# Eight routed experts: pairs of experts in turn, transposes a step late, outputs by 128 slots, weights in two rings

## The chip, the cores and the metric

The kernel runs on one core of a Trainium2 chip. The metric is device time in microseconds; lower is better. The unmodified kernel took 2508.5 us in the median of three runs (2505.13 to 2510.0). Engines are named as in the profile: PE (matmul), PEld (its weight loads), DVE, ACT, POOL, and SP, whose queue issues the loads of weights from HBM.

## The reference, cut to what matters

The program is a two-layer block followed by a second block of other kinds of layers. The change touches one part, the mixture of experts of 256 tokens with 1024 features:

```
logits = h @ w_router;  top_val, top_idx = lax.top_k(logits, 2);  top_w = softmax(top_val)
gates = sum(one_hot(top_idx, 8) * top_w[..., None], axis=-2)
for e in range(8):
    y = (silu(h @ w_gate[e]) * (h @ w_up[e])) @ w_down[e]      # 1024 -> 3584 -> 1024
    out = out + gates[..., e:e+1] * y
```

All weights are fp32. The eight experts have 8 x 3 x 1024 x 3584 x 4 bytes = 352.3 MB, and each byte is read once.

## The kernel before, in words

The router sorts the experts by how many tokens chose them (`sort`) and gives each place p of 0 to 7 a fixed number of slots, `CAPS` = 96, 64, 96, 64, ... A branch on the largest count covers the case that a place overflows; in these inputs it isn't taken. `gather` copies the tokens of some places into slots, with one-hot matrices as matmul operands. Place 0 is always expert 0, whose weights stand at a known address; the addresses of the others are read at run time, after the sort.

Weights come as 42 blocks of 1 MiB per expert, 128 partitions by 2048 fp32. The first 28 hold gate and up columns, in four steps (8, 8, 8 and 4 blocks), and the last 14 hold the down projection. `Ahead` issues the loads on SP in the order of use, and `next` keeps ten blocks loaded or on the way (L239-244). A block has one of ten homes in turn (L227): eight are tiles of two pools with four buffers each ("raw" and "hl", which the other stages use for weights too), loaded in one piece of 1 MiB (L230); two are four units each of the general pool of 52 units of 128 x 512, loaded in four pieces of 256 KB (L235). A load waits on SP until PE has read the block that had its home before.

`expert` works on one place at a time. A group is 32 slots, so a place has three groups or two. In a step, PE multiplies the group's slots by four column tiles of the block: two tiles of gate columns into partitions 0 to 63 of a bank, two of up columns into 64 to 127 (L977). The first two groups have banks of the pool "mm", the third one of the pool "ax"; each pool has four. Then, for each group, ACT takes silu of the gate half (L983), DVE multiplies by the up half (L984), PE transposes 64 x 128 pieces (L990), and ACT or DVE copies the result to a unit (L994, L996), which is the down projection's operand (L1010). At the end ACT and DVE copy the outputs to Y (L1018, L1020), PE multiplies Y by the transposed gate matrix pT, eight matmuls of fp32, and DVE adds to the stream x (L1026). `experts` takes the places in sets, 0, then 1 to 3, 4 and 5, 6 and 7, and gathers the next set within the down projection before it. Pieces of the second block's preparation (`block2_context`) are hung on steps of the places 6 and 7 (`todo`).

A scheduler sets the order on each engine from the program's order, priorities and free buffers. Each engine then runs in that order.

Of the kernel before, what the change touches and what calls it, by code (L numbers as in the profile page):

```python
# [8 lines left out]
F32 = mybir.dt.float32  # L9
F32R = mybir.dt.float32r  # L10
# [3 lines left out]
AF = mybir.ActivationFunctionType  # L14
ALU = mybir.AluOpType
AX = mybir.AxisListType
# [14 lines left out]
RAWB, HLB = 4, 4  # L31
# [107 lines left out]
class Weights:  # L139


    def __init__(self):
        self.at, self.items, self.size = {}, [], 0
# [68 lines left out]
class Ahead:  # L212


    def __init__(self, K, off, homes=10, depth=10):
        self.K, self.off, self.loaded, self.used = K, off, [], 0
        self.homes, self.depth = homes, depth
        self.n = K.wts.experts()[1] // (P * CH)

    def fill(self, n):  # L220
        K = self.K
        while len(self.loaded) < min(n, NE * self.n):
            i = len(self.loaded)
            p, c = divmod(i, self.n)
            o = self.off[p] + c * P * CH
            src = K.a["wts"][bass.ds(o, P * CH)].rearrange("(p n) -> p n", p=P)
            home = (i + self.homes - 8) % self.homes  # L227
            if home > 1:
                t = K.wp.tile([P, CH], F32, name=K.nm("raw"), tag="raw" if home % 2 else "hl", bufs=RAWB if home % 2 else HLB)
# [9 lines left out]
    def next(self):  # L239
        i = self.used  # L240
        self.used += 1
        self.fill(i + self.depth)
        out, self.loaded[i] = self.loaded[i], None
        return out


class Kern:
# [578 lines left out]
    def moe(self, x):  # L826
# [68 lines left out]
        ahead = Ahead(self, [first] * NE)  # L895
        held = ahead.fill(8)
# [7 lines left out]
        with tc.If(n > 0):  # L904
            self.experts(x, hth, htl, srt, Ahead(self, begins, 2, 3), 0)
            self.experts(x, hth, htl, srt, Ahead(self, begins, 2, 3), 1)
            for u in [rt[:, 0]] + self.cx.u + held:
                nc.vector.tensor_copy(u[:, :1], u[:, :1])
        self.experts(x, hth, htl, srt, ahead)
# [31 lines left out]
    def experts(self, x, hth, htl, srt, ahead, over=None):  # L941
# [7 lines left out]
        nxt = None  # L949
        for i, places in enumerate(sets):  # L950
            if nxt is None:
                with self.tc.high_priority(offset=self.hp if over is None else 0):
                    nxt = self.gather(places, caps, base, hth, htl, srt)
            cur, nxt = nxt, None
            for p in places:
                last = p == places[-1] and i + 1 < len(sets)
                for s in self.expert(x, *cur[p], ahead):
                    if over is None and (p, s) in todo:
                        self.block2_context(*todo[p, s])
                    if s == 3 and last:  # L960
                        nxt = self.gather(sets[i + 1], caps, base, hth, htl, srt)

    def expert(self, x, slots, xg, pT, ahead):

        nc = self.nc
        groups = slots // GS
        ge = lambda g: slice(g * GS, g * GS + GS)
        hT = []
        for s, (a, w, kc) in enumerate(steps()):
            pss = [self.psm() if g < 2 else self.psx() for g in range(groups)]  # L970
            for k0 in range(0, KD, kc):
                blocks = ahead.next()
                for k in range(k0, k0 + kc):
                    for g in range(groups):
                        for q in range(4):
                            o = ((k - k0) * 4 + q) * w
                            self.nc.tensor.matmul(pss[g][q * GS:(q + 1) * GS, :w], xg(k, g),  # L977
                                                  blocks[o // 512][:, o % 512:o % 512 + w], start=k == 0,
                                                  stop=k == KD - 1, tile_position=(0, q * GS))
            nb, hs = w // P, [None] * groups  # L980
            for g in range(groups):
                sg, ht = self.tmp()[64:, :w], self.tmp()[64:, :w]
                nc.scalar.activation(sg, pss[g][:64, :w], AF.Silu)  # L983
                nc.vector.tensor_mul(ht, pss[g][64:, :w], sg)  # L984
                if g % 2 == 0:
                    pt, u = self.psx(), self.unit(name="hT")
                    n = min(groups - g, 2) * nb * 64
                at = (g % 2) * nb * 64
                for b in range(nb):
                    nc.tensor.transpose(pt[:, at + b * 64:at + b * 64 + 64], ht[:, b * P:(b + 1) * P],  # L990
                                        self.ident[64:, 64:])
                if g % 2 or g == groups - 1:
                    if g < 2:
                        nc.scalar.activation(u[:, :n], pt[:, :n], AF.Copy)  # L994
                    else:
                        nc.vector.tensor_copy(u[:, :n], pt[:, :n])  # L996
                hs[g] = u[:, at:at + nb * 64]
            for c in range(2):
                for b in range(nb):
                    hT.append([h[:, b * 64 + c * GS:b * 64 + c * GS + GS] for h in hs])  # L1000
            yield s
        ya, yb = self.psm(), self.psx() if groups > 2 else None
        y = [(ya, ya, yb)[g][:, (g % 2) * 256:(g % 2) * 256 + 256] for g in range(groups)]
        for k0 in range(0, EDIM // P, 2):
            blocks = ahead.next()
# [7 lines left out]
        Y = [self.unit(name="Y") for _ in range(2)]  # L1013
        for g in range(groups):
            for q in range(4):
                dst, src = Y[q // 2][ge(g), (q % 2) * 256:(q % 2) * 256 + 256], y[g][q * GS:(q + 1) * GS]
                if q % 2:
                    nc.scalar.activation(dst, src, AF.Copy)  # L1018
                else:
                    nc.vector.tensor_copy(dst, src)  # L1020
# [6 lines left out]
        yield len(steps())  # L1027

    def gather(self, places, caps, base, hth, htl, srt):

        nc = self.nc
        io = self.c["iota"]
# [3 lines left out]
        pg = self.unit(name="pg")[:, :2 * n].rearrange("p (t s) -> p t s", t=2)  # L1036
        for p in places:
            r, c = RANKS[p], caps[p]
            pos = srt[:, 4:6, r:r + 1]
            if base[p]:  # L1040
                pos = self.small(2)[:, :, None]
                nc.vector.tensor_scalar(pos, srt[:, 4:6, r:r + 1], -float(base[p]), None, op0=ALU.add)
            for dst, row in ((pr, 0), (pg, 2)):
                for t in range(2):
                    nc.vector.tensor_scalar(dst[:, t, at[p]:at[p] + c], io[:, :c], pos[:, t], srt[:, row + t, r:r + 1],
                                            op0=ALU.is_equal, op1=ALU.mult)
# [14 lines left out]
        out = {}  # L1061
        for i, p in enumerate(places):
            c = caps[p]
            if i % 2 == 0:
                ps, pT = self.psx(), self.unit(name="pT")
                two = places[i:i + 2]
            for t in range(2):
                nc.tensor.transpose(ps[:c, (i % 2) * T + t * P:(i % 2) * T + (t + 1) * P], pg[:, t, at[p]:at[p] + c], self.ident)
            o = slice((i % 2) * T, (i % 2) * T + T)
            nc.vector.tensor_copy(pT[:c, o], ps[:c, o])  # L1070
            out[p] = (c, lambda k, g, a=at[p]: xg[k][:, a + g * GS:a + g * GS + GS], pT[:, o])
        return out
# [744 lines left out]
```

## Time and profile before

| | us |
|---|---|
| median of three runs | 2508.5 |
| the profiled execution | 2513.52 |
| its span, first to last instruction | 2511.7 |
| PE busy in the span | 2389.0 |
| DVE, ACT, POOL busy | 1124.6, 812.1, 96.3 |

The page gives busy times, and a busy PE is not one at its peak, since matmuls overlap. What limits a stage is read from the chain of waits and from the share of the DMA engines by stretches: at 1.0 all 16 have packets all the time. The mean granted TensorE clock of the execution is 0.978, where 1.00 is the upper of two levels, 2.4 GHz, and 0.50 the lower. Names such as mm and ax are banks that matmuls write, raw is a block of weights, whl the split weights of the other stages, xg gathered tokens, hT the transposed hidden values.

### The profile page before, as it was taken

To read this page: it belongs to the slowest core of one execution; us is meant where nothing else is said; L and a number is where in the kernel's file an instruction comes from. 1 tells how busy PE (TensorE), PEld (TensorE's weight loads), DVE (VectorE), ACT (ScalarE), POOL (GpSimd) and SP (SyncE) were. 2 spreads that over 40 slices of the span, in tenths; PEclk is the share of its full clock that TensorE was granted. 3 is DMA by queue.
4 is the path that set the end of the run, shared out by engine and by line. 5 is a ranking of instruction groups with operands and counts; after the bars stand their busy time and mean duration, and the time that the engine had idled before them with its cause. 6 is when DMAs were issued, how large, how long until landed. Compare 5 with 4: busy or idle time off the path is not lost.

```text
span 2511.7 us, 47630 instructions
## 1 busy us (share of the span) xinstructions
PE 2389.0 (95%) x20181; PEld 1708.9 (68%) x20181; DVE 1124.6 (45%) x2262; ACT 812.1 (32%) x1372; POOL 96.3 (4%) x96
## 2 busy tenths in 40 slices
PE   8999999979989999999999998999899999898998
PEld 6788888743533535354343688878788888778998
DVE  5475545721101011111111256966764454786884
ACT  5544433611000010100101255332442342464663
POOL 0000001000000000000011100000100000101000
PEclk9999999989999999999999999999899999998999
DMA  8468787469999999999999821111222322222552
GB/s 307 175 239 291 275 290 259 161 255 361 348 409 408 390 404 398 411 397 405 381 395 405 320 84 51 42 55 66 90 74 103 117 80 88 89 101 68 193 186 93
DMA packets 113341, 581.80 MB, mean 232 GB/s; under 512 B 12727, under 2 KB 12983, under 8 KB 54368
## 3 DMA queue, kind: packets, MB, share of 16 engines
q1 hardware_dynamic: 111456, 572.74, 60.0%
q0 software_dynamic: 1664, 5.93, 0.7%
q8 instruction: 160, 2.62, 0.4%
q14 instruction: 61, 0.50, 0.1%
HBM read 575.48 MB, written 3.15 MB: 230 GB/s over the span
## 4 chain that ended last, share of the span: by engine, by line
PE 66%; DMA 4%; DVE 4%; issue 2%; ACT 2%; POOL 1%; SPq 0%; DVEq 0%; ACTq 0%; POOLq 0%
PE mm L302 32%; PE mm L977 14%; PE ax L302 6%; PE mm L1010 5%; DMA raw<-in_wts 4%; PE ax L977 4%; PE ax L1010 2%; PE ax L990 1%; DVE whl L359 0%; DVE t L984 0%; PE ax L1741 0%; ACT t L983 0%; DVE x L1140 0%; DVE t L421 0%; SPq L230 0%
## 5 line engine op out<-in xcount | busy, mean ns | idle before, releaser
L302 PE MATMUL mm<-h,whl 128*128 128x256 f32 (+2 forms) x3280 | 718.6, 314 | 14.7 <-ACT whl L358 12.2
L302 PEld LDWEIGHTS mm<-h,whl 128*128 128x128 f32 (+1 forms) x3280 | 537.1, 189 | 79.8 <-issue 23.7
L302 PE MATMUL mm<-l,whl 128*128 128x256 f32 (+2 forms) x1640 | 510.6, 313 | 0.0
L977 PE MATMUL mm<-raw,xg 128*32 128x512 f32 (+1 forms) x4096 | 488.4, 546 | 5.9 <-DMA raw<-in_wts 5.9
L359 DVE TENSOR_TENSOR whl<-raw,whl 128x1024 fp32r<-128x1024 f32 (+4 forms) x314 | 367.6, 1177 | 250.9 <-ACT whl L358 250.6
L358 ACT ACTIVATE whl<-raw 128x1024 fp32r<-128x1024 f32 (+4 forms) x314 | 318.6, 1021 | 292.7 <-PE mm L302 261.5
L977 PEld LDWEIGHTS mm<-raw,xg 128*32 128x32 f32 x4096 | 152.4, 111 | 256.9 <-issue 213.0
L302 PEld LDWEIGHTS mm<-l,whl 128*128 128x128 f32 (+1 forms) x1640 | 308.2, 188 | 20.0 <-issue 0.3
L1010 PE MATMUL mm<-raw,hT 128*32 128x256 f32 x3584 | 253.1, 385 | 10.7 <-DMA raw<-in_wts 10.6
L302 PE MATMUL mm<-fh,whl 128*128 128x256 f32 (+1 forms) x1056 | 236.1, 318 | 0.0
L984 DVE TENSOR_TENSOR t<-mm,t 64x512 f32<-64x512 f32 (+1 forms) x64 | 39.8, 627 | 436.0 <-ACT t L983 435.7
L1010 PEld LDWEIGHTS mm<-raw,hT 128*32 128x32 f32 x3584 | 135.2, 111 | 94.9 <-DMA raw<-in_wts 19.9
L983 ACT ACTIVATE t<-mm 64x512 f32<-64x512 f32 (+1 forms) x64 | 33.8, 534 | 498.0 <-PE mm L977 470.4
L302 PEld LDWEIGHTS mm<-fh,whl 128*128 128x128 f32 x1056 | 174.2, 188 | 21.5 <-issue 4.2
L977 PE MATMUL ax<-raw,xg 128*32 128x512 f32 (+1 forms) x1024 | 173.5, 541 | 0.0
L302 PE MATMUL mm<-fl,whl 128*128 128x256 f32 (+1 forms) x528 | 167.2, 317 | 0.0
L1020 DVE COPY Y<-mm 32x256 f32<-32x256 f32 x32 | 13.3, 416 | 225.7 <-PE mm L1010 218.7
L1010 PE MATMUL ax<-raw,hT 128*32 128x256 f32 x896 | 111.3, 379 | 0.0
L302 PEld LDWEIGHTS mm<-fl,whl 128*128 128x128 f32 x528 | 98.9, 187 | 7.7
L302 PE MATMUL mm<-f,whl 128*128 128x256 f32 (+1 forms) x732 | 97.8, 290 | 1.4 <-ACT f L358 1.4
L302 PEld LDWEIGHTS mm<-f,whl 128*128 128x128 f32 x732 | 91.0, 188 | 5.5 <-ACT f L358 2.0
L977 PEld LDWEIGHTS ax<-raw,xg 128*32 128x32 f32 x1024 | 48.3, 110 | 63.2 <-issue 56.6
(447 smaller groups left out, 2495.7 us busy)
## 6 DMA issues: line engine op xcount, KB each, us to landing
raw<-in_wts SPq DMA_DIRECT2D x458, 1024.0 KB, 7.1
raw<-in_wts SPq DMA_DIRECT2D x268, 256.0 KB, 9.0
raw<-in_wts SPq DMA_DIRECT2D x8, 768.0 KB, 4.5
raw<-in_wts SPq DMA_DIRECT2D x12, 512.0 KB, 3.4
raw<-in_wts SPq DMA_DIRECT2D x8, 384.0 KB, 3.0
raw<-in_wts SPq DMA_DIRECT2D x4, 576.0 KB, 3.7
spill<-x POOLq DMA_DIRECT2D x8, 256.0 KB, 3.3
x<-spill POOLq DMA_DIRECT2D x8, 256.0 KB, 4.0
```

The lines of the kernel that those rows point to most:

```text
L302: self.nc.tensor.matmul(out, lhsT, rhs, start=start, stop=stop)
L358: self.nc.scalar.activation(hi, src, AF.Copy)
L359: self.nc.vector.tensor_sub(lo, src, hi.bitcast(F32))
L977: self.nc.tensor.matmul(pss[g][q * GS:(q + 1) * GS, :w], xg(k, g), blocks[o // 512][:, o % 512:o % 512 + w], start=k == 0, stop=k == KD - ...
L983: nc.scalar.activation(sg, pss[g][:64, :w], AF.Silu)
L984: nc.vector.tensor_mul(ht, pss[g][64:, :w], sg)
L990: nc.tensor.transpose(pt[:, at + b * 64:at + b * 64 + 64], ht[:, b * P:(b + 1) * P], self.ident[64:, 64:])
L1010: self.nc.tensor.matmul(y[g][q * GS:(q + 1) * GS], hT[k][g], blocks[o // 512][:, o % 512:o % 512 + 256], start=k == 0 and g != 1, stop=k = ...
L1020: nc.vector.tensor_copy(dst, src)
```

## The change

- Places are taken in pairs (0, 1), (2, 3), (4, 5), (6, 7). The four steps of both alternate (`passes`), in the first pair with place 1 a step behind; the two down projections follow one another. The blocks are loaded in this order (`loads`).
- Blocks are kept in the two rings of four only. The early loads, before the branch, are eleven instead of eight; blocks 8 to 10 go to units. `next` keeps eight blocks ahead.
- The second group's gate and up halves change places in the bank (r = q ^ 2), so that the hidden values of groups 0 and 1 fill one tile of 128 partitions. It is transposed by 128 x 128 matmuls, and the transposes of a step stand behind the matmuls of the next one.
- Outputs of the places are collected in tiles of 128 slots (640 slots, five tiles). `combine` makes the gate matrix of a tile, turns it into a gain per slot and a 0/1 matrix, scales Y, splits it into a high and a low half of type fp32r, and multiplies both, 16 matmuls of one pass.

```diff
-RAWB, HLB = 4, 4
+RAWB, HLB, AHEAD = 4, 4, 3
-        ahead = Ahead(self, [first] * NE)
-        held = ahead.fill(8)
+        pairs = [(p, p + 1) for p in range(0, NE, 2)]
+        ring = lambda i: None if 8 <= i < 8 + AHEAD else ("raw", "hl")[(i - AHEAD * (i >= 8)) % 2]
+        ahead = Ahead(self, [first] * NE, loads(passes(pairs)), ring, 8)
+        held = ahead.fill(8 + AHEAD)
...
+def passes(pairs):
+    out = []
+    for i, pair in enumerate(pairs):
+        n = len(steps())
+        if len(pair) == 1:
+            out += [(pair[0], s) for s in range(n)]
+        else:
+            lag = 1 if i == 0 else 0
+            a, b = pair
+            for s in range(n + lag):
+                out += [(a, s)] * (s < n) + [(b, s - lag)] * (s >= lag)
+        out += [(p, None) for p in pair]
+    return out
...
-        todo = {(6, 0): (1,), (6, 1): (2,)}
-        for k in range(0, KD, 2):
-            todo[divmod(27 + k // 2, 4)] = (3, [k, k + 1])
-        sets = ([0], [1, 2, 3], [4, 5], [6, 7]) if over is None else [[p, p + 1] for p in range(0, NE, 2)]
...
+            todo = {(7, 0): [(1,)], (6, 2): [(2,)], (7, 2): [(3, (0, 1))], (6, 3): [(3, (2, 3))], (7, 3): [(3, (4, 5))],
+                    (6, None): [(3, (6, 7))]}
...
+        for i, (p, s) in enumerate(passes(sets)):
+            mine = next(j for j, places in enumerate(sets) if p in places)
+            if s is not None:
+                ps = self.gate_up(p, s, caps[p] // GS, xgs[p], ahead)
+                new = self.hidden(s, caps[p] // GS, ps, hT.setdefault(p, []))
+            else:
+                new = None
+                for part in self.down(p, caps[p] // GS, hT[p], ahead):
+                    if part == 1 and after:
+                        after()
+                        after = None
+                y = part
+            if after:
+                after()
+            after = new
+            if s is None:
+                hT.pop(p)
+                self.collect(y, at[p], caps[p] // GS, Y)
+                if p == sets[mine][0] and mine + 1 < len(sets):
+                    xgs = {**xgs, **self.gather(sets[mine + 1], caps, base, hth, htl, srt)}
+                xgs = {q: v for q, v in xgs.items() if q != p}
+                end = at[p] + caps[p] if p == NE - 1 else at[p + 1]
+                while done < end // P or (p == NE - 1 and done in Y):
+                    self.combine(done, x, Y.pop(done), caps, base, at, srt)
+                    done += 1
...
+            gate, up = (slice(64, P), slice(0, 64)) if g == 1 else (slice(0, 64), slice(64, P))
+            nc.scalar.activation(sg[up], pss[g][gate, :w], AF.Silu)
+            nc.vector.tensor_mul(ht[up], pss[g][up, :w], sg[up])
...
+                    if both:
+                        nc.tensor.transpose(pt[:, b * P:b * P + P], ht[:, bs], self.ident)
                     else:
+                        nc.tensor.transpose(pt[:, b * 64:b * 64 + 64], ht[64:, bs], self.ident[64:, 64:])
...
+        nc.vector.tensor_reduce(gs, ps[:n, :T], axis=AX.X, op=ALU.add)
+        nc.vector.tensor_scalar(pT, ps[:n, :T], 0.0, None, op0=ALU.is_gt)
+        yh = [self.unit(F32R, "yh")[:n] for _ in range(2)]
+        yl = [self.unit(F32R, "yl")[:n] for _ in range(2)]
+        for h, l, y in zip(yh, yl, Y):
+            nc.scalar.activation(h, y[:n], AF.Copy, scale=gs)
+            nc.vector.scalar_tensor_tensor(l, y[:n], gs, h.bitcast(F32), op0=ALU.mult, op1=ALU.subtract)
...
-                self.mm(ps[:, q * T:(q + 1) * T], Y[m // 4][:slots, (m % 4) * P:(m % 4 + 1) * P], pT[:slots])
+                self.mm(o, yh[m // 4][:, ms], pT, start=True, stop=False)
+                self.mm(o, yl[m // 4][:, ms], pT, start=False, stop=True)
             nc.vector.tensor_add(u, ps, u)
```

On SP's queue, around the branch, before: the last early load, the reads of the sort's result (place), the branch, and the first pieces behind it.

```order
L230 DMA raw_5332<-in_wts 128x2048
L899 TENSOR_LOAD place
L897 TENSOR_LOAD place
L899 TENSOR_LOAD place x6
L904 COMPARE_AND_BRANCH
L235 DMA raw_5434<-in_wts 128x512
```

And after the change; five more rows like the first, and the last early load of 1 MiB, stand ahead of these.

```order
L235 DMA raw_5345<-in_wts 128x512
L235 DMA raw_5346<-in_wts 128x512
L235 DMA raw_5347<-in_wts 128x512
L235 DMA raw_5352<-in_wts 128x512
L235 DMA raw_5353<-in_wts 128x512
L235 DMA raw_5354<-in_wts 128x512
L235 DMA raw_5355<-in_wts 128x512
L925 TENSOR_LOAD place
L927 TENSOR_LOAD place x7
L932 COMPARE_AND_BRANCH
```

Twelve pieces for the blocks 8 to 10 moved ahead of the reads and the branch; the rows behind it in the file are those of the branch that isn't taken.

On PE, the end of the first expert's second step, before: t is the hidden values of one group, ax the bank that its transposes write, and raw_25518 the next step's first block.

```order
L977 MATMUL mm_25563<-raw_25504,xg_25396 32x512 x4
L977 MATMUL ax_25564<-raw_25504,xg_25396 32x512 x4
L990 MATMUL ax_25693<-cst,t_25690 128x64 x4
L977 MATMUL mm_25719<-raw_25518,xg_25381 32x512
L990 MATMUL ax_25693<-cst,t_25700 128x64 x4
L977 MATMUL mm_25719<-raw_25518,xg_25381 32x512 x3
L990 MATMUL ax_25712<-cst,t_25709 128x64 x4
L977 MATMUL mm_25720<-raw_25518,xg_25381 32x512 x4
```

And after: ht_25800 is the hidden values of groups 0 and 1 of the step before, ht_25806 those of group 2, and the block behind them is place 1's first.

```order
L1024 MATMUL mm_25810<-raw_25812,xg_25690 32x512 x4
L1024 MATMUL ax_25811<-raw_25812,xg_25690 32x512 x4
L1051 MATMUL ax_25934<-cst,ht_25800 128x128 x4
L1053 MATMUL ax_25941<-cst,ht_25806 128x64 x4
L1024 MATMUL mm_25948<-raw_25826,xg_25664 32x512 x4
L1024 MATMUL mm_25949<-raw_25826,xg_25664 32x512 x4
```

Three sets of four transposes became two, and they belong to the step before the one that just ended.

On PE, where place 6 begins, before: the first two groups' last block of the step, the combine of place 5 (pT and Y), and then the third group's matmuls of the step's first block, raw_30605.

```order
L977 MATMUL mm_30805<-raw_30739,xg_30492 32x512
L977 MATMUL mm_30806<-raw_30738,xg_30492 32x512
L977 MATMUL mm_30806<-raw_30739,xg_30492 32x512
L302 MATMUL ax_30789<-pT_28707,Y_30779 128x256 x2
L302 MATMUL ax_30793<-pT_28707,Y_30779 128x256 x2
L302 MATMUL ax_30797<-pT_28707,Y_30780 128x256 x2
L302 MATMUL ax_30801<-pT_28707,Y_30780 128x256 x2
L977 MATMUL ax_30807<-raw_30605,xg_30466 32x512 x4
L977 MATMUL ax_30807<-raw_30623,xg_30466 32x512 x4
```

And after, where place 6 begins: the end of the down projection before it and its own first two blocks.

```order
L1077 MATMUL mm_30362<-raw_30471,hT_29942 32x256 x16
L1024 MATMUL mm_30623<-raw_30489,xg_30290 32x512 x4
L1024 MATMUL mm_30624<-raw_30489,xg_30290 32x512 x4
L1024 MATMUL ax_30625<-raw_30489,xg_30290 32x512 x4
L1024 MATMUL mm_30623<-raw_30507,xg_30290 32x512 x4
L1024 MATMUL mm_30624<-raw_30507,xg_30290 32x512 x4
L1024 MATMUL ax_30625<-raw_30507,xg_30290 32x512 x4
```

The third group's matmuls now follow each block, and the combine stands elsewhere, within a down projection.

## Rows read from the trace of the kernel before

**Rows 1.** Busy time by stretches (us, instructions), granted clock, DMA share, GB/s.

```profile
core 0: us, PE busy (x) PEld busy (x) DVE busy (x) ACT busy (x) POOL busy (x), PEclk, DMA share, GB/s
543.00:690.00 147.00, 146.38 (x1722) 64.39 (x1718) 19.76 (x43) 14.80 (x29) 0.00 (x0) 1.00 0.92 352
690.00:840.00 150.00, 139.61 (x1488) 53.63 (x1484) 15.57 (x26) 13.27 (x25) 0.00 (x0) 0.99 1.02 409
840.00:920.00 80.00, 79.30 (x1089) 38.96 (x1084) 8.23 (x16) 5.54 (x13) 0.00 (x0) 1.00 1.00 392
...
1106.00:1220.00 114.00, 104.99 (x1147) 46.55 (x1139) 14.80 (x32) 11.79 (x25) 0.00 (x0) 1.00 1.02 406
1220.00:1240.00 20.00, 20.00 (x161) 6.70 (x163) 4.29 (x7) 4.44 (x8) 5.49 (x5) 1.00 0.83 330
...
700.00:1400.00 700.00, 669.45 (x7880) 293.50 (x7883) 80.91 (x165) 68.87 (x140) 30.92 (x36) 0.99 1.01 400
```

**Rows 2.** The chain of waits: start us, length us, what.

```profile
532.56 7.03 PE ax L302 x32
...
540.04 3.57 PE mm L977 x16
543.61 1.23 PE ax L977 x8
...
547.42 1.72 PE mm L977 x16
549.13 0.86 PE ax L977 x8
...
1191.04 20.06 DMA raw<-in_wts
```

**Rows 3.** Issues of SP's queue: start, length in us, line, what.

```profile
509.75 1.69 SPq L230 DMA_DIRECT2D raw<-in_wts  x2
...
532.23 4.79 SPq L235 DMA_DIRECT2D raw<-in_wts  x8
544.91 18.35 SPq L230 DMA_DIRECT2D raw<-in_wts  x8
```

**Rows 4.** Packets, 519 to 533 us; loads from 544, median us to landing.

```profile
DMA packets 96, 0.39 MB, mean 28 GB/s; under 512 B 13, under 2 KB 13, under 8 KB 87
...
raw<-in_wts SPq DMA_DIRECT2D x6, 1024.0 KB, 4.8
```

**Rows 5.** Packets landed: 800 to 814, 818 to 822, 1029 to 1033 us.

```profile
DMA packets 807, 5.87 MB, mean 419 GB/s; under 512 B 92, under 2 KB 92, under 8 KB 92
DMA packets 751, 1.55 MB, mean 387 GB/s; under 512 B 85, under 2 KB 85, under 8 KB 721
DMA packets 737, 1.58 MB, mean 396 GB/s; under 512 B 84, under 2 KB 84, under 8 KB 697
```

**Rows 6.** Who waited for whom: total us, times, longest us.

```profile
DVE pr L1045 <- SPq L904: 5.9, 1, 5.9
...
SPq L230 <- PE ax L977: 145.3, 68, 9.2
```

**Rows 7.** Timeline of PE around 1217 us and at the stage's end.

```profile
1217.68 3.72 PE L302 MATMUL ax<-pT,Y 64*128 64x256 f32 x16
...
1395.87 0.81 PE L990 MATMUL ax<-cst,t 64*128 64x64 f32 x4 [5.17 <-DVE t L984]
1396.62 26.51 PE L1010 MATMUL mm<-raw,hT 128*32 128x256 f32 x448
1423.06 0.29 PE L302 MATMUL mm<-h,whl 128*16 128x256 f32 x1
1423.18 0.28 PE L302 MATMUL mm<-l,whl 128*16 128x256 f32 x1
```

**Rows 8.** Two stretches of 20 us, columns as in rows 1.

```profile
740.00:760.00 20.00, 16.23 (x233) 7.98 (x237) 0.83 (x2) 0.52 (x2) 0.00 (x0) 0.91 1.03 408
...
1180.00:1200.00 20.00, 15.59 (x244) 7.59 (x240) 1.16 (x3) 0.75 (x2) 0.00 (x0) 1.00 1.02 404
```

More of the change, by code (lines that the diff above doesn't have):

```diff
@@ L244, in next, with loads @@
         return out
+def passes(pairs):
[11 more added lines that the diff above has]
+    return out
+def loads(todo):
+    first, at = [], 0
+    for a, w, kc in steps():
+        first.append(range(at, at + KD // kc))
+        at += KD // kc
+    return [(p, c) for p, s in todo for c in (range(at, at + EDIM // P // 2) if s is None else first[s])]
 class Kern:
@@ L939, in sort, with experts @@
         return srt, place
-    def experts(self, x, hth, htl, srt, ahead, over=None):
+    def experts(self, x, hth, htl, srt, sets, ahead, over=None):
         caps = CAPS if over is None else (CAPS[0],) * NE
         base = [0 if over is None else CAPS[p] + over * CAPS[0] for p in range(NE)]
-        todo = {(6, 0): (1,), (6, 1): (2,)}
-        for k in range(0, KD, 2):
-            todo[divmod(27 + k // 2, 4)] = (3, [k, k + 1])
-        sets = ([0], [1, 2, 3], [4, 5], [6, 7]) if over is None else [[p, p + 1] for p in range(0, NE, 2)]
[L949 to L961, printed above, removed]
@@ new lines, in experts @@
+        at = [sum(caps[:p]) if over is None else p * P for p in range(NE)]
+        hp = self.hp if over is None else 0
+        todo = {}
+        if over is None:
+            todo = {(7, 0): [(1,)], (6, 2): [(2,)], (7, 2): [(3, (0, 1))], (6, 3): [(3, (2, 3))], (7, 3): [(3, (4, 5))],
+                    (6, None): [(3, (6, 7))]}
+        with self.tc.high_priority(offset=hp):
+            xgs = self.gather(sets[0], caps, base, hth, htl, srt)
+        hT, after, Y, done = {}, None, {}, 0
+        for i, (p, s) in enumerate(passes(sets)):
[23 more added lines that the diff above has]
+                    done += 1
+            for job in todo.get((p, s), ()):
+                self.block2_context(*job)
@@ new lines, in gate_up @@
+    def gate_up(self, p, s, groups, xg, ahead):
+        a, w, kc = steps()[s]
+        first = sum(KD // steps()[i][2] for i in range(s))
+        pss = [self.psm() if g < 2 else self.psx() for g in range(groups)]
+        for k0 in range(0, KD, kc):
+            blocks = ahead.next((p, first + k0 // kc))
+            for k in range(k0, k0 + kc):
+                for g in range(groups):
+                    for q in range(4):
+                        o = ((k - k0) * 4 + q) * w
+                        r = q ^ 2 if g == 1 else q
+                        self.nc.tensor.matmul(pss[g][r * GS:(r + 1) * GS, :w], xg(k, g),
+                                              blocks[o // 512][:, o % 512:o % 512 + w], start=k == 0,
+                                              stop=k == KD - 1, tile_position=(0, r * GS))
+        return pss
@@ L1002, in expert, with down @@
+    def down(self, p, groups, hT, ahead):
+        first = sum(KD // kc for _, _, kc in steps())
         ya, yb = self.psm(), self.psx() if groups > 2 else None
         y = [(ya, ya, yb)[g][:, (g % 2) * 256:(g % 2) * 256 + 256] for g in range(groups)]
-        for k0 in range(0, EDIM // P, 2):
-            blocks = ahead.next()
+        for i, k0 in enumerate(range(0, EDIM // P, 2)):
+            blocks = ahead.next((p, first + i))
             for k in range(k0, k0 + 2):
@@ L1060, in gather @@
             xg += [u[:, k * n:k * n + n] for k in range(kn)]
[L1061 to L1072, printed above, removed]
+        return {p: lambda k, g, a=at[p]: xg[k][:, a + g * GS:a + g * GS + GS] for p in places}
     def rms_out(self, x, gain):
```

134 lines of the change are left out of this document (71 added, 63 removed).

## The prediction

> **What bounds the kernel now.** The page shows PE busy for 95% of the span, which would make PE the bound everywhere. The table by stretches corrects this for the expert stage, which runs from 540 to 1423 us. In 700 to 1400 us the DMA share is 1.01 and the rate 400 GB/s; of the stretches shown after 690 us only 1220 to 1240 is below 1.00, while PE's idle time grows to 9 us in 114 [rows 1]. So the stage is bound by its loads: 336 blocks of 1 MiB (8 experts of 42), 352.3 MB in all.
>
> The chain of waits says the same from PE's side. A block for three groups of 32 slots costs PE 1.72 + 0.86 = 2.58 us, one for two groups 1.72 us; around 1191 us the chain stands on a landing weight block for 20 us [rows 2]. At 400 GB/s a block of 1.0486 MB lands every 2.62 us. A 96-slot expert therefore keeps PE just level with the loads and falls behind by all that is not matmul; a 64-slot expert waits.
>
> There are three leaks in the load stream. First, from 543 to 690 us the rate is 352 GB/s [rows 1]: the first expert has 96 slots, all ten homes are full, and each load waits until PE frees one. Second, the last of the 8 early loads is issued at 511 us, and from 519 to 533 us 0.39 MB moves; the first load behind the branch starts at 532.2 [rows 3, 4]. Third, two of every ten blocks go to units in pieces of 256 KB. In 800 to 814 us, where no packet is 2 KB long, the rate is 419 GB/s, 2.50 us a block; in 818 to 822 and 1029 to 1033, where nearly all data packets are, 387 and 396, which is 2.68 us [rows 5]. Four parts of the one and one of the other make 2.54 us. The stage's 2.62 is 0.08 above that; in the stretches where PE waits most, 409 and 406 GB/s or 2.57 us, it is only 0.03 [rows 1].
>
> **The change, part by part.**
>
> *Two rings only.* 66 of the 336 blocks come in pieces today, three after the change. The rest has 8 KB packets, and the clean rate becomes 2.50 us a block. What lies above it I bound by the rows: 0.03 (where PE waits) to 0.08 (the mean). I take 0.055, between the two, because the waiting stretches become longer but not all of the stage: 2.555 us. The depth falls from ten blocks to eight, 20.4 us of loads.
>
> *Eleven early loads.* The 12 pieces for blocks 8 to 10 stand on SP ahead of the branch. DVE's first instruction behind the branch waited for SP there [rows 6], so late pieces would delay the stage. They queue behind the load issued at 511 us; three blocks in pieces need 8 us from about 519, so they land by 528, before the 532 us at which SP now issues behind the branch [rows 3]. They fill the idle stretch and cost nothing; were they held up, each us is a us, and I allow up to 5.
>
> *Interleaved pairs.* In the first pair expert 0 runs two steps alone, 16 blocks. Start: the gather now has 160 columns instead of 96 and three more one-hot operations ahead of it; before, it took 7.03 us [rows 2], and I allow 0.7 us more, so PE starts at 540.7. The first block takes 4.9 us at the lower clock (540.04 to the first refill at 544.91) [rows 2, 3], 15 more take 2.58, the first step's 8 transposes 1.6: 585.9. A two-group block then frees the home of block 24 at 587.6. A load that finds the queue empty lands 4.8 us after its issue [rows 4]: 592.4. Until there loads go at PE's pace; while PE uses blocks 8 to 10, which free no ring home, they pause, and this is in the sum. From there PE frees homes every 1.72 us in the two-group steps and the loads have no gap.
>
> Does it stay so? A pair needs of PE 42 x (2.58 + 1.72) = 180.6 us, a gather 7.0, 42 transposes at about 0.2 (four took 0.81 [rows 7]) 8.5, and 1.25 combines. A combine has 16 matmuls on split halves, which no row shows in this place; the nearest are 0.12 us apart (the next stage's, on the same type) and 0.46 (3.72 us for the 8 of today's combine, written as 16 rows) [rows 7]. So it takes 2 to 7 us plus two transposes. Sum 199 to 206 us, against 84 x 2.555 = 214.6 us of loads. The least slack is 9 us a pair, and within a pair PE is at most about 6 of 8 blocks behind. I price PE's work at nothing from 592.4 on; the loads cover it.
>
> *Transposes a step later, for two groups at once.* Today PE stands still at the step's end until ACT and DVE are done; then the transposes have their operands a step early. By the loops they go from 280 to 168. This is PE's time, which the loads hide: zero, except in the first 52 us, where the sum has it already.
>
> *Outputs by 128 slots.* Five combines instead of eight, and DVE's four additions to x per combine also five times. In today's order the third group's matmuls of a new expert stand behind the combine, so homes stay occupied; SP waited up to 9.2 us for them, 145 us in all [rows 6], and 1220 to 1240 us lost 3 to 4 us to it (330 GB/s) [rows 1]. The combine now stands inside the two-group down projection, and the third group follows its block at once. I still leave 3 us for one such stop, since the context's jobs sit in the last pair.
>
> *The end.* Loads: 592.4 + 311 x 2.555 = 1387. Last block 1.72 us plus a short wait: 1389. Before, the last expert matmul ends at 1423.1, where the next stage's begin at once [rows 7], because PE had run the last down projection at its own pace, 26.5 us for 14 blocks. So PE gains 34 us. Now the next stage's weights land only behind the last block and must be split by ACT and DVE while these also collect outputs: I take 3 us of the gain away, bounds 0 and 6.
>
> Sum: -34 + 3 + 3 = -28 us. The profiled execution took 2513.5 us with a span of 2511.7; the median of the runs is 2508.5, 5 us less. The stages behind are the same work in the same order, so I apply the difference to the median: 2480.5 us.
>
> **Where a page speaks against the rows.** From 800 to 814 us 5.87 MB landed, 419 GB/s [rows 5]. The Trainium skill, "DMA: Bandwidth & Descriptors", Specifications, puts what one core gets from HBM at about 358 GB/s; by that the stage could not be under 984 us before or after and the packets' size would be worth nothing. The trace does not agree: this core ran above it.
>
> **Rivals.**
>
> *The rate does not rise.* If the blocks in pieces were never what held the stream, a block keeps its 2.62 us. For: the excess of 0.08 over the clean mix shows that something else slows it, and 840 to 920 us, where PE is densest, has only 392 GB/s at a share of 1.00 [rows 1]. Against: 409 and 406 in two long stretches. Then 311 x 0.065 = 20 us of the gain go: -8 us, 2500.5.
>
> *PE falls to the lower clock (slower).* With loads as the bound, PE waits at every two-group block, 0.8 of 2.56 us. If the granted clock fell to 1.2 GHz there, a two-group block would take 3.44 us, longer than a load. A pair would need 42 x (2.58 + 3.44) + 19 = 272 us instead of 214.6, 57 us more, four times: 2711 us. It turns into a loss once the low clock holds longer than about 130 us in the stage: half of that is the gain of 28 and the pairs' slack of 36. Against: at 740 to 760 us, PE busy 16.2 of 20 us, the clock was 0.91, and at 1180 to 1200, with 15.6 busy, 1.00 [rows 8]; the 0.91 is 3.6 us at the lower level, and it came back. The Trainium skill, "TensorE: Matmul & The Clock Gate", HAM oscillation, tells of a kernel where each wait for a load put the array back to the low clock; by that rule this case would be the likely one. The rows bear it out only for single short falls.
>
> *Start and end eat it.* Late pieces at the branch (5 us) and the full 6 us of refill at the end, with the upper rate bound of 2.58: -34 + 8 + 5 + 6 + 3 = -12 us, 2496.5.
>
> **How the numbers follow.** Forecast 0.64, its own range 2463 to 2492 (rate 2.52 and no losses at the end: -45; rate 2.58 with the allowances: -20, with a little noise). Rate does not rise 0.14; start and end 0.10; lower clock 0.05; other effects of the order, such as a unit or bank missing and PE standing behind it, 0.07, of which 0.03 slower and 0.01 the same. This kernel's measurement tells 0.2%, 5 us, from no change. The two cases of a smaller gain end within 5 us in a third of their cases. So faster 0.83, the same 0.09, slower 0.08. The range, 2462 to 2501, leaves out the slower cases and the far side of both ends.
>
> **What would show it.** Right: the DMA share at 1.0 from about 590 us to the end of the stage, no data packets of 2 KB behind the start, 408 to 415 GB/s; the chain of waits standing on landing weights in the two-group steps; the stage's last expert matmul near 1389 us. Wrong: a rate near 400 with 8 KB packets only; SP waiting for PE in the middle of the stage; a granted clock well below 0.98 between 600 and 1390; a stretch after 590 us in which the DMA share is below 0.95 for 20 us.

## The result, and the profile after

The changed kernel took 2476.7 us in the median of four runs (2476.21 to 2481.29), the kernel before 2507.3; the ratio is 0.9881, 95% interval 0.9864 to 0.9899. That is 30.6 us less; the forecast was 28 less, 2480.5. In a second set of runs the changed kernel came to 2478.3 and 0.9870 (0.9853 to 0.9888). The profiled execution took 2481.3 us, 32.2 less than that of before.

The stretches of [rows 1] in the changed kernel, and the whole stage from 592 us on, with the same columns:

```profile
543.00:592.00 49.00, 49.00 (x460) 14.23 (x456) 4.57 (x7) 4.13 (x7) 0.00 (x0) 1.00 0.81 321
...
543.00:690.00 147.00, 143.60 (x1618) 53.01 (x1614) 13.93 (x24) 15.09 (x28) 0.00 (x0) 1.00 0.95 386
690.00:840.00 150.00, 141.90 (x1666) 59.44 (x1662) 18.55 (x39) 14.36 (x28) 0.00 (x0) 0.99 1.01 418
840.00:920.00 80.00, 75.33 (x1104) 36.64 (x1100) 7.20 (x16) 7.40 (x15) 0.00 (x0) 1.00 1.01 418
...
930.00:950.00 20.00, 19.75 (x319) 11.98 (x322) 5.04 (x10) 2.04 (x4) 0.00 (x0) 1.00 0.92 366
...
592.00:1378.00 786.00, 744.42 (x9406) 328.89 (x9402) 96.66 (x211) 85.69 (x171) 31.21 (x36) 1.00 1.01 416
```

The reader is to see three things. Until 592 us loads still go at PE's pace (share 0.81, 321 GB/s). From there to the end the share is 1.01 and the rate 416 to 418 GB/s in the long stretches; 840 to 920, which had 392 before, no longer stands out. One short stretch does: from 930 to 950 us the share is 0.92 and the rate 366 GB/s, about one block (2.5 us) less than at 418. PE has a gather and a combine within the pair's down projections there, and SP waits up to 6.2 us for a home. And the granted clock is 1.00, the upper level, although PE waits.

The packets of 592 to 1378 us and of 800 to 814:

```profile
DMA packets 44828, 326.67 MB, mean 416 GB/s; under 512 B 4968, under 2 KB 5032, under 8 KB 5032
...
DMA packets 801, 5.87 MB, mean 420 GB/s; under 512 B 85, under 2 KB 85, under 8 KB 85
```

"Under 8 KB" and "under 2 KB" are the same count, so no packet of 2 KB is left, and the clean rate is that of [rows 5]. The Trainium skill, "DMA: Bandwidth & Descriptors", Specifications, lists about 358 GB/s as the limit of one core from HBM; in this kernel, which runs on one core, the trace holds 416 for 786 us, and the measurement decides.

The chain of waits (start, length, what), in the place of [rows 2]:

```profile
540.18 2.77 PE mm L1024 x16
...
646.28 13.24 DMA raw<-in_wts
...
661.56 19.46 DMA raw<-in_wts
...
809.85 14.87 DMA raw<-in_wts
```

From 646 us the chain keeps standing on a landing block. Before, it did so in three places, from 719, 957 and 1165 us on; now it does in every pair. The end of the stage, the timeline of PE beside [rows 7]:

```profile
1379.23 1.93 PE L1077 MATMUL mm<-raw,hT 128*32 128x256 f32 x32 [0.55 <-DMA raw<-in_wts]
1381.78 1.94 PE L1077 MATMUL mm<-raw,hT 128*32 128x256 f32 x32 [0.61 <-DMA raw<-in_wts]
1383.64 0.29 PE L328 MATMUL mm<-h,whl 128*16 128x256 f32 x1
```

Before, PE ran its last 14 blocks without a wait. Now it waits for each of the last four (two are shown), and the next stage begins at 1383.6 instead of 1423.1: 39.4 us earlier. Of these 32.2 reach the end; where the rest stays is told with the prediction's steps.

### The profile page after: what moved, and what is told of

Read it like the earlier page. It is cut to its first block, busy times and chain, and to the rows that moved or that the text cites. A ratio compares the mean times of both kernels' runs of the same rounds, so it can differ in the third digit from the quotient of the medians.

```text
span 2479.5 us, 46633 instructions
## 1 busy us (share of the span) xinstructions
PE 2342.2 (94%) x20015; PEld 1683.1 (68%) x20015; DVE 1125.4 (45%) x2271; ACT 819.3 (33%) x1382; POOL 96.9 (4%) x96
## 4 chain that ended last, share of the span: by engine, by line
PE 61%; DMA 11%; DVE 4%; ACT 1%; issue 1%; DVEq 0%; ACTq 0%
PE mm L328 33%; DMA raw<-in_wts 11%; PE mm L1024 10%; PE ax L328 6%; PE mm L1077 6%; PE ax L1024 4%; PE ax L1077 2%; DVE whl L385 0%; DVE Y L1094 0%; PE ax L1051 0%; PE ax L1829 0%; DVE x L1228 0%; DVE sm L490 0%; DVE t L447 0%; DVE sm L495 0%
## 5 line engine op out<-in xcount | busy, mean ns | idle before, releaser
L1024 PE MATMUL mm<-raw,xg 128*32 128x512 f32 (+1 forms) x4096 | 430.9, 543 | 28.0 <-DMA raw<-in_wts 27.9
L1024 PEld LDWEIGHTS mm<-raw,xg 128*32 128x32 f32 x4096 | 129.9, 110 | 281.3 <-issue 179.9
L1041 DVE TENSOR_TENSOR ht<-mm,t 64x512 f32<-64x512 f32 (+1 forms) x64 | 39.8, 622 | 485.6 <-ACT t L1040 484.1
L1077 PE MATMUL mm<-raw,hT 128*32 128x256 f32 x3584 | 223.5, 381 | 9.4 <-DMA raw<-in_wts 8.3
L1077 PEld LDWEIGHTS mm<-raw,hT 128*32 128x32 f32 x3584 | 114.3, 110 | 90.3 <-DMA raw<-in_wts 13.7
L1024 PE MATMUL ax<-raw,xg 128*32 128x512 f32 (+1 forms) x1024 | 126.3, 539 | 0.0
L1092 ACT ACTIVATE Y<-mm 32x256 f32<-32x256 f32 x32 | 12.0, 375 | 223.9 <-DVE Y L1094 223.4
L1220 DVE SCALAR_TENSOR_TENSOR t<-mm,par,t 128x510 f32<-128x510 f32 (+1 forms) x88 | 53.8, 614 | 66.9 <-ACT t L1217 66.9
## 6 DMA issues: line engine op xcount, KB each, us to landing
raw<-in_wts SPq DMA_DIRECT2D x521, 1024.0 KB, 13.2
```

Source lines behind the costliest of these rows:

```text
L1024: self.nc.tensor.matmul(pss[g][r * GS:(r + 1) * GS, :w], xg(k, g), blocks[o // 512][:, o % 512:o % 512 + w], start=k == 0, stop=k == KD - ...
L1041: nc.vector.tensor_mul(ht[up], pss[g][up, :w], sg[up])
L1077: self.nc.tensor.matmul(y[g][q * GS:(q + 1) * GS], hT[k][g], blocks[o // 512][:, o % 512:o % 512 + 256], start=k == 0 and g != 1, stop=k = ...
L1092: self.nc.scalar.activation(dst, src, AF.Copy)
L1220: nc.vector.scalar_tensor_tensor(o3[:, :, 1:], p3[:, :, :T - 1], w(0), o3[:, :, 1:], op0=ALU.mult, op1=ALU.add)
```

## The experiments

Ratios are to the kernel before in the same rounds. A diff shows the lines that matter of what differs from the kernel named; in e3, e6, e7 and e12 the jobs in `todo` also move, to steps at about the same place in the sequence.

| run | median us | ratio (95%) |
|---|---|---|
| e1 old order, rings only | 2517.7 | 1.0038 (1.0026 to 1.0051) |
| e2 new order, a fifth in pieces | 2488.2 | 0.9920 (0.9904 to 0.9937) |
| e3 steps of a pair one after the other | 2481.9 | 0.9894 (0.9878 to 0.9910) |
| e4 eight early loads | 2478.0 | 0.9880 (0.9861 to 0.9898) |
| e5 transposes not delayed | 2481.5 | 0.9879 (0.9860 to 0.9898) |
| e6 place by place | 2503.2 | 0.9973 (0.9965 to 0.9982) |
| e7 place by place, not delayed | 2514.5 | 1.0017 (1.0005 to 1.0028) |
| e8 six blocks held | 2471.3 | 0.9848 (0.9832 to 0.9864) |
| e9 old order, eight ahead | 2509.0 | 0.9999 (0.9989 to 1.0008) |
| e10 five blocks held longer | 2467.1 | 0.9827 (0.9814 to 0.9839) |
| e11 changed kernel again | 2478.3 | 0.9870 (0.9853 to 0.9888) |
| e12 place by place, ten homes | 2490.7 | 0.9922 (0.9908 to 0.9935) |

**Packets, in the new order (e2).**

```diff
+if i % 5 == 0 and i > 10:
+    for j in range(4):
+        K.nc.sync.dma_start(t[:, j * 512:(j + 1) * 512], src[:, j * 512:(j + 1) * 512])
+else:
     K.nc.sync.dma_start(t, src)
```

> The changed kernel, with each fifth block behind the eleventh loaded by four DMAs of 256 KB into the same ring home: order, homes and depth stay, only the packets of 65 blocks go from 8 to 2 KB. Theory A: 65 x 0.18 = 12 us more than the changed kernel, about 2489 us, the rate between 592 and the end of the stage 2.57 us a block instead of 2.54. Rival B: no change, 2477 us.

It took 11.5 us more than the changed kernel's first median, 10 more than its second. Its packets from 592 to 1378 us:

```profile
DMA packets 70597, 321.97 MB, mean 410 GB/s; under 512 B 7832, under 2 KB 7832, under 8 KB 39216
```

410 GB/s instead of 416 with order and homes alike, so the price of 0.18 us for a block in pieces holds, and rival B falls. The edit changes the size of the packets and the number of DMAs together; which of the two costs is not shown.

**Packets, in the old order (e1).**

```diff
-ahead = Ahead(self, [first] * NE)
+ahead = Ahead(self, [first] * NE, 8, 8)    # and every block in the rings
```

> The kernel before with the order of work as it was, but all blocks in the two rings of four: no block in pieces, eight homes and eight ahead. Theory A (66 blocks lose their 2 KB packets, worth 0.18 us each, and the order keeps whatever else slowed the stream): 66 x 0.18 = 12 us less, about 2496 us, last expert matmul near 1411. Rival B (the packets' size is worth nothing, the order is all): 2508, last matmul near 1423. Rival C (in the old order the loads need ten homes, because the third group's matmuls hold them in the 96-slot experts): slower than before, 2515 or more.

Rival C came true: 10 us slower than before. The stretch 840 to 905 us lies in place 2 of the old order, with 96 slots. Its row in e1, then in the changed kernel, columns as in [rows 1]:

```profile
840.00:905.00 65.00, 63.60 (x922) 32.87 (x914) 8.24 (x16) 5.54 (x13) 0.00 (x0) 1.00 0.94 372
```

```profile
840.00:905.00 65.00, 60.34 (x845) 28.09 (x841) 7.20 (x16) 7.40 (x15) 0.00 (x0) 1.00 1.01 418
```

The loads issued in the same stretch, with the median us from issue to landing at the end of the row, in e1 and in the changed kernel:

```profile
raw<-in_wts SPq DMA_DIRECT2D x25, 1024.0 KB, 7.3
```

```profile
raw<-in_wts SPq DMA_DIRECT2D x25, 1024.0 KB, 17.0
```

A load into an empty queue lands after 4.8 us [rows 4]. A median of 7.3 says that the queue is nearly dry, one of 17.0 that loads stand in line, and the DMA share of 0.94 against 1.01 says the same. The kernel before has in this stretch:

```profile
840.00:905.00 65.00, 64.47 (x956) 33.94 (x948) 7.42 (x15) 4.69 (x12) 0.00 (x0) 1.00 1.00 387
```

Its whole blocks land after a median of 7.2 us, so the old order's queue was short with ten homes already. With eight the rate falls from 387 to 372 GB/s although every block is whole: the old order starves its loads, and more is lost than the packets give.

**Where the order counts (e3, e6, e7, e12).** e3 keeps the pairs, but runs the four steps of one place and then those of the other; e6 works each place off whole:

```diff
-lag = 1 if i == 0 else 0
+lag = n                                            # e3
```

```diff
-for s in range(n + lag):
-    out += [(a, s)] * (s < n) + [(b, s - lag)] * (s >= lag)
-out += [(p, None) for p in pair]
+for p in pair:                                     # e6, e7, e12
+    out += [(p, s) for s in range(n)] + [(p, None)]
```

> The changed kernel without interleaving: in each pair the four steps of the 96-slot place, then the four of the 64-slot place, then the two down projections; all else stays, the jobs of the second block's preparation hang on the same positions. Theory A (eight homes hold 20 us of loads, and PE falls behind by at most about 10 us in 28 blocks of a 96-slot place, so that only the first pair's start suffers, 12 more blocks at PE's pace): 3 to 5 us more than the changed kernel, about 2481. Rival B (the old order's 0.045 us a block above the changed kernel's comes from sequence): 311 x 0.045 = 14 us more, about 2491.

> The changed kernel with each place worked off whole, as in the old order: its four steps, its down projection, then the next place; delayed transposes, new outputs, gathers by pairs and the rings stay. Theory E (what counts is how far PE falls behind in one run of 96-slot blocks against the 20 us that eight homes hold: 42 blocks x 0.04 + 6 of transposes + a gather of 7 and a combine of 3 is about 18 us, so it just holds behind the first place): 0 to 8 us more than with the steps apart but the down projections together (2482), 2482 to 2490. Rival B (working place by place is what made the old order slow with rings): about the 2518 of the old order with rings, at least 2505.

e3 came as theory A says, 3.7 us above e11, and its loss lies in the first pair: 403 GB/s from 592 to 690 us, where the changed kernel has 418, but 416 against 415 from 690 to 1106. e6 was outside theory E's 2482 to 2490 and 2 us under rival B's bound. So a run of 28 blocks of the 96-slot place is carried by eight homes, and one of 42 is not. The same stretch in e6:

```profile
840.00:905.00 65.00, 64.75 (x821) 31.83 (x825) 10.84 (x25) 6.63 (x14) 0.00 (x0) 1.00 0.87 337
```

PE is busy to the brim and the loads stand. My 18 us for PE's lag was too small. e12 gives the two homes back, pieces and all:

```diff
-ring = lambda i: None if 8 <= i < 8 + AHEAD else ("raw", "hl")[(i - AHEAD * (i >= 8)) % 2]
+ring = lambda i: None if i % 10 >= 8 else ("raw", "hl")[i % 2]    # and AHEAD = 2, ten ahead
```

> The place-by-place run with the changed kernel's code (2503 us), but with the old ten homes: two of ten blocks in units, in pieces of 256 KB, eight in the rings. Theory E (its 26 us over the changed kernel come from eight homes that hold 20 us of loads while PE falls some 26 behind in 42 blocks of a 96-slot place; ten homes hold 25): the stops at the ends of the 96-slot places go and the pieces' 12 us come, 2492 to 2498 us, fewer loads in the 96-slot places landing 5 us after their issue. Rival F (the number of homes doesn't matter): 2503 + 12 = 2515 us.

```profile
840.00:905.00 65.00, 65.00 (x822) 31.79 (x818) 11.40 (x26) 7.72 (x16) 0.00 (x0) 1.00 1.02 408
```

From 337 to 408 GB/s in this stretch and 12.5 us less in all, although a fifth of the blocks comes in pieces again at some 11 us. That is 1 us below theory E's range. If the pieces cost here what they cost in e2, two homes are worth about 24 us to this order (12.5 and the 11); rival F falls in any case. With ten homes the order itself matters little: e12 is 2.5 us above e2, the interleaved order with as many pieces and eight homes. And e12 has the homes, the share of pieces and the order of places of the kernel before, yet is 20 us faster than it (0.9922): so much do the delay, the shared transposes, the new outputs, the gathers by pairs and two more early blocks give together when there are ten homes. e7 takes the delay away too:

```diff
-if after:
-    after()
-after = new
+if new:
+    new()
```

> As the run before, and the transposes at their own step's end as well: the old order with rings, with the new outputs and shared transposes only. Theory E (both together bring PE behind by more than eight homes hold): 2505 to 2518, loads landing 5 us after their issue within the 96-slot places. Rival (the old combine with its 16 fp32 passes, 3.7 us, and the third group's matmuls behind it made the old order slow): as the run before, 2482 to 2490.

11 us more than e6, in theory E's range, and by the ratios only 5 us under e1. What the new outputs, the shared transposes and the gathers by pairs give together in this order, with eight homes, is therefore small beside the delay and the interleaving.

**The delay, in pairs (e5).** The same edit in the changed kernel.

> The changed kernel with the transposes of a step issued at that step's own end, pairs interleaved as they are. Theory A (the loads set the stage; each pair leaves PE about 9 us, and a 64-slot step stands behind each 96-slot step to take up what PE loses): 0 to 5 us more than the changed kernel, 2477 to 2482. Rival D (the delay is what keeps PE level with the loads; without it PE stands some 3 us at each of 32 step ends, 96 us, of which the slack hides 36): up to 60 us more, 2537; and already 2490 would speak for it.

PE's longest waits between 543 and 1420 us (total, times, longest), in e5 and then in the changed kernel:

```profile
PE ax L1050 <- DVE ht L1040: 15.3, 24, 1.4
PE mm L1023 <- DMA raw<-in_wts: 12.7, 21, 1.5
PE mm L1076 <- DMA raw<-in_wts: 3.6, 6, 1.0
```

```profile
PE mm L1024 <- DMA raw<-in_wts: 27.9, 47, 2.1
PE mm L1077 <- DMA raw<-in_wts: 8.3, 13, 2.1
```

In e5 the transposes wait for DVE, 15 us, and the matmuls wait 20 us less for the loads. The time is the same within the intervals (3 us above e11): the slack of a pair takes it up, and rival D falls. The delay is worth 11 us in one order (e6 and e7) and next to nothing in the other.

**Early loads (e4).** `AHEAD = 0`.

> The changed kernel with eight early loads instead of eleven. Theory A (from 592 us on the loads have no gap and set the end, so each block that lands before the branch is worth its 2.5 us): 7.5 us more, about 2484 us, last expert matmul near 1391. Rival C (PE, not the loads, sets the end of the stage; the loads have slack): no change, 2477 us.

I was wrong here. The time doesn't change, though three blocks less lie ready at the branch. In e4 the stretch from 543 us reads:

```profile
543.00:592.00 49.00, 49.00 (x460) 14.13 (x456) 4.57 (x7) 4.14 (x7) 0.00 (x0) 1.00 0.94 373
```

373 GB/s against 321: e4 simply catches up. Until 592 us PE sets the pace and the loads stand at what PE has used plus the ring's eight, in either kernel. The three units are empty again by then. PE was not the stage's end, as rival C has it; the blocks were early in a stretch that doesn't count.

**Blocks that are still held when it counts (e8, e10).** Both load blocks out of turn into units, three ahead of the branch and the rest right behind it:

```diff
-RAWB, HLB, AHEAD = 4, 4, 3
+RAWB, HLB, AHEAD, HELD = 4, 4, 3, range(24, 30)    # e8; e10: range(40, 45)
-ahead = Ahead(self, [first] * NE, loads(passes(pairs)), ring, 8)
+ahead = Ahead(self, [first] * NE, loads(passes(pairs)), ring, 8, HELD)   # these right behind the first eight
...
+ahead.fill(8 + len(HELD))
 self.experts(x, hth, htl, srt, pairs, ahead)
```

> The changed kernel with other early blocks: instead of blocks 8 to 10, which PE uses up before it outruns the loads, six blocks of the first expert's third step (24 to 29), three ahead of the branch and three right behind it, all in units; they stay until PE comes to them at about 600 us. Theory A, corrected by the eight early loads that cost only 1.3 us (until 586 us PE sets the pace and the loads stand at what it has used plus the ring's eight; only a home that is still full at that time counts): six blocks are worth 6 x 2.54 = 15 us, less than the three times 9 us that PE has to spare in the later pairs: last expert matmul at about 1368, 2462 us. Rival C (PE has no room left and sets the end): 2470 to 2477.

e8 gave some 7 us, not 15, and its time lies where rival C put it. The trace names another cause. What moved from 600 to 616 us, in 40 slices:

```profile
GB/s 451 410 389 512 369 430 389 451 410 389 512 369 430 389 451 410 389 471 389 451 307 164 82 82 0 0 0 0 0 0 0 0 0 0 0 0 0 0 0 0
```

While PE works through the six held blocks no ring home comes free, the rings are full, and the loads stop.

> The changed kernel with five blocks in units instead of the three, held longer than the six were: the four blocks of the first expert's last step and the next block of place 1 (40 to 44), three loaded ahead of the branch, two right behind it, used from about 640 us on. Theory G (the six of before were used up at 600 to 615 us, while PE was still behind and no ring home came free, so the loads stopped there, 372 GB/s from 592 to 690; from about 640 on PE waits for loads, and a block that is still held then is worth its whole 2.54 us): 13 us less than the changed kernel, 2464 us, last expert matmul near 1371, 416 GB/s or more from 592 to 690. Rival C (PE has no room left, or units run short and the loads stop): 2470 or more.

```profile
592.00:690.00 98.00, 98.00 (x1258) 44.10 (x1254) 9.36 (x17) 10.96 (x21) 0.00 (x0) 1.00 0.99 405
```

And the next stage's first matmul, in the timeline of PE:

```profile
1373.46 0.29 PE L330 MATMUL mm<-h,whl 128*16 128x256 f32 x1
```

2467.1 us, 11 less than e11 in the same rounds, where 13 were expected; the next stage begins at 1373.5 instead of 1385.4. The stop is smaller, but not gone (405 GB/s, where 416 or more were expected; e8 had 372). Rival C falls: PE had the room. This version beats both kernels.

> The changed kernel once more, on the same chip and in the same rounds as the runs beside it: 2477 us, last expert matmul at 1384.

**A run that did not test its theory (e9).** `Ahead(self, [first] * NE, 10, 8)` in the kernel before.

> The kernel before as it was, ten homes and pieces and order, but loads go only eight blocks ahead of PE's use instead of ten. Theory E (in the old order the run of 42 blocks of a 96-slot place brings PE behind by more than eight blocks hold, so that two homes fewer were what cost the old order with rings its 12 us and 10 more): 2518 to 2530 us, loads in the 96-slot places landing 5 us after their issue. Rival F (the rings made the old order slow by something else than their number): 2508, as before.

2509.0, no change, which by the letter speaks for rival F. But the number only says where in the program's order a load is written. SP issues it once its home is free, and the homes stayed ten: whole blocks issued between 840 and 905 us land after 7.2 us in e9 as in the kernel before. e12 put the question rightly.

## Why the prediction was right

*The place.* The loads bound the stage, and what made it shorter is a higher rate and a stream with hardly a gap. Both parts are in the table of stretches.

*The packets.* 311 blocks at 2.50 plus an allowance. The clean part holds (420 GB/s, and e2). The allowance was too large: the last block's matmuls start at 1381.8, so a block cost, counted from the forecast's 592.4, (1381.8 - 592.4) / 311 = 2.538 us against 2.555, and 5.3 us of the forecast end go to that. The row of the stretches where PE waits (0.03) was the right one; the mean of the stage (0.08) held the stops of the 96-slot places, which the interleaving removes. Seen from there, "the rate does not rise" had the right suspicion, something besides the packets, and the wrong conclusion.

*The depth.* I let eight blocks for ten pass without a price. In the new order it has none; in the old one two homes are worth more than the packets. The steps between the kernels can be walked in runs: rings alone in the old order +0.38%; new outputs, shared transposes and gathers by pairs -0.21; the delay -0.44; the interleaving -1.0 (e6 to the mean of the two sets, 0.9876). At 2509 us that is about +10, -5, -11 and -24 us. None of these is the worth of an edit by itself: with ten homes the interleaving has little to cure (e12), and in pairs the delay has nothing to give (e5). I had priced the delay and the outputs at nothing and the higher rate, for the packets' sake, at most of the gain (311 x 0.065 = 20 us). e2 gives the pieces 10 to 11.5 us. The other 20 of the 31 come with the pieces still in place, whether by interleaving with eight homes (e2, 0.9920) or place by place with ten (e12, 0.9922), and what e12 has over the kernel before is mostly what I had put at nothing. The sum came out because the cures overlap; that it came within 3 us is in part luck.

*The start.* First expert matmul at 540.2 (forecast 540.7), and from 592 us the loads run at the full rate, as forecast. The early pieces cost nothing: DVE's first instruction behind the branch waited as long as before [rows 6].

```profile
DVE pr L1135 <- SPq L932: 6.0, 1, 6.0
```

*Within the stage.* The stop behind a combine, for which the sum left 3 us, came from 930 to 950 us and cost about 2.5; PE's work was thus not quite at nothing, as I had priced it. But these 2.5 are already in the 2.538, so the 3 us were not needed beside it. So the last expert matmul ended 8 us earlier than the 1392 that the sum held.

*The signs.* Two of my signs of being wrong came up all the same. From 592 us on SP waits for PE all through the stage (total us, times, longest us; the largest row):

```profile
SPq L230 <- PE ax L1024: 219.1, 95, 8.9
```

Yet the loads of this time land after a median of 16.4 us, so they stand in line, and a wait of SP for a home costs nothing while the queue is full: the sign was badly chosen. The other, a share below 0.95 for 20 us, is the stop at 930, and real.

*The end.* I gave back 3 us for the next stage's weights. A row that both kernels have some 40 us behind the boundary, in the kernel before and then in the changed one:

```profile
1459.32 0.35 DVE L1320 RECIPROCAL gdng<-gdng 128x32 f32<-128x32 f32 x1 [0.88 <-ACT gdng L1318]
```

```profile
1423.00 0.35 DVE L1408 RECIPROCAL gdng<-gdng 128x32 f32<-128x32 f32 x1 [1.33 <-ACT gdng L1406]
```

36.3 us apart, where the boundary is 39.4: 3.1 us given back. What the sum did not hold is 4 us more, lost 200 us later in a stage of its own (last section): -39.4 + 3.1 + 4 = -32, the difference of the profiled spans (2511.7 and 2479.5).

*The lower clock.* Rival with 5 in 100. PE now waits for loads, 36 us in the stage (27.9 and 8.3, shown with e5), 0.6 us at a time and 2.1 at most, and from 592 to 1378 us the mean granted clock is 1.00; in the one stretch of 20 us where it is lower, 730 to 750, it is 0.91 (PE busy 14.4 of 20 us). The Trainium skill, "TensorE: Matmul & The Clock Gate", HAM oscillation, tells of a kernel that fell to the low clock at each wait for a load; its waits were several times as long as these 0.6 us. I read it too widely when I called this case the likely one by it, and the trace neither confirms nor refutes it.

*What one profile is worth.* The execution of before that the prediction reads took 2513.5 us, 5 above its median. e9, whose loads wait for the same homes, has runs from 2500.5 to 2515.8, and its profiled one (the shortest) reaches the next stage at 1413.6 instead of 1423.1. The 39 us are thus those of one pair of executions; the 30.6 between medians is the result. The changed kernel's eight runs lie between 2474.8 and 2482.5.

## What to carry to other kernels

A stage that streams weights is judged by the gaps of its load stream, and a gap has two cures, more homes or an order in which the consumer never falls behind by more than the homes hold; price an edit by what is left after the others. Interleaving a heavy with a light consumer needs fewer homes than taking them in turn (42 heavy blocks in a row broke eight homes, 28 did not). A block that is loaded early is worth its transfer only if its home is still full when the loads begin to set the pace, and only if the others don't all stand full while it is used up (three gave nothing, six gave 7 us, five held longer 11).

## What the runs showed of the hardware that was not expected

A stage that the change doesn't touch took 4 us longer in the profiled execution. It is a chain of short matmuls and DVE operations, and both kernels run it in the same order. The same DVE operation of it in the kernel before and then in the changed one:

```profile
1660.45 1.23 DVE L1509 TENSOR_TENSOR u<-u,ax 64x128 f32<-64x128 f32 x4 [0.56 <-PE ax L302]
```

```profile
1627.97 1.23 DVE L1597 TENSOR_TENSOR u<-u,ax 64x128 f32<-64x128 f32 x4 [1.68 <-PE ax L328]
```

Here they stand 32.5 us apart, where the rows at 1459 and 1423 stood 36.3. Twenty microseconds ahead of it, columns as in [rows 1]:

```profile
1640.00:1660.00 20.00, 19.74 (x134) 16.02 (x132) 10.31 (x33) 6.02 (x10) 3.18 (x6) 0.83 0.31 105
```

```profile
1605.00:1625.00 20.00, 19.95 (x112) 15.27 (x113) 7.52 (x26) 5.34 (x9) 3.06 (x6) 0.67 0.25 81
```

The clock falls to the lower level in this stage in both, for about 6.8 us of these twenty before (0.17 of 20 us, times two, since the lower level is half) and 13.2 after. That is a matter of the execution and not of the change. Between two DVE operations of this chain, the later of them the one shown, PE runs the same 96 matmuls in every kernel. This stretch in the changed kernel, in its second profiled execution (e11), in the kernel before and in e9:

```profile
1610.02:1627.97 17.95, 17.94 (x96) 13.24 (x94) 6.79 (x25) 2.43 (x5) 0.00 (x0) 0.62 0.14 48
```

```profile
1611.66:1625.36 13.70, 13.49 (x96) 10.25 (x94) 6.79 (x24) 2.43 (x5) 0.00 (x0) 0.88 0.20 69
```

```profile
1646.70:1660.45 13.75, 13.54 (x96) 10.23 (x94) 6.79 (x25) 2.42 (x5) 0.00 (x0) 0.88 0.17 63
```

```profile
1636.03:1648.22 12.19, 11.98 (x96) 8.94 (x94) 6.79 (x25) 2.42 (x5) 0.00 (x0) 1.00 0.14 51
```

The other profiles have one of these three lengths too: 12.2 us at 1.00 (e1, e2, e6, e7, e8), 13.7 at 0.88 (e10) and 17.9 at 0.62 (e3, e4, e5, e12). The changed kernel alone has two of them. So the length goes with the clock, and the 4 us are the difference between two falls. What decides which fall an execution gets is not shown.
